# Weight sums for sixteen later Strassen squares made beside the attention and kept in DRAM

## The chip, the cores and the metric

The kernel runs on one core of a Trainium2 chip. The metric is device time of one execution in microseconds (us). The kernel before took 2009.71 us, the median of three runs (2009.61 to 2010.11). About 0.2% (4 us) is what a measurement of this kernel can tell from no change.

## The reference, cut to what matters

One transformer block over 256 tokens of width 4096, in float32:

```python
h = rmsnorm(x, norm_w)
u = h @ w_in                       # mLSTM q,k,v,o,z and attention q,k,v,gates,z
y_ml = mlstm(conv(u)) * sigmoid(ml_o) * silu(ml_z)
y_ns = sparse_attention(u) * silu(ns_z)
x = x + concat(y_ml, y_ns) @ w_out
x = x + sigmoid(x @ ple_gate) * (p @ ple_proj)
```

Nearly all of the arithmetic is in the products of 256 x 4096 activations with weight matrices of 4096 rows. The weights are read from DRAM once.

## The kernel before, in words

**Three matmuls for each product.** TensorE takes a rounded float32 type, so each operand is split into a rounded part and the rest. For a weight tile `raw`, ScalarE (ACT) writes the rounded part `whi` (line L1542) and VectorE (DVE) writes `wlo` = `raw` - `whi` (L1543). Activations lie split in SBUF as `sh` and `sl`, the stationary operands. A product is whi x sh, whi x sl and wlo x sh, all issued at L1256.

**Units.** The weights come in tiles of 128 x 2 x 512 floats (512 KB). The program is a queue of *units*, one tile each. While TensorE (PE) works on unit n, ACT and DVE split unit n + 3 (`LOOK = 3`). `whi` and `wlo` have four buffers each, `raw` has six (`RAWB = 6`). Loads of `raw` are issued on the SyncE queue (L1532) in the order of the units, each as soon as one of the six tiles is free; a tile is free when DVE has written its `wlo`.

**Groups and plans.** 1024 output columns (pairs of 512) make a group; it has 16 steps, one for each pair of 128-row blocks `kp`. Groups P1 to P5 are input projections, -6 to -1 the gates, 0 to 3 multiply by `w_out`, 4 to 7 by `ple_gate`. `PLANS[g]` writes out the order of a group's steps by hand. A step is of one of two kinds:

- `C`, plain: two units of 12 matmuls, 24 in all.
- *mixed square*: a Strassen-like 2 x 2 block product with seven block products in place of eight: four units `a1`, `a2`, `c1`, `c2` of 3, 6, 6 and 6 matmuls, 21 in all. Unit `a1` splits half a tile (L1549 on ACT, L1550 on DVE). Units `c1` and `c2` split sums of the same two raw tiles; DVE makes the sums in place with four adds of 128 x 512 (L1343, L1344, L1346, L1347), so both tiles stay held until `c1` and `c2` are split. The order is `a1 a2 C C' c1 c2`: a plain step stands between, and two of the four adds follow each of its splits. Below, "m/C" is such a mixed square with its plain step, and 3/2 is the mixed square of kp 3 with the plain step of kp 2.

A mixed square also needs *mixed* activations (sums of activation blocks), stationary tiles of their own that `t_mix` or `t_stat` makes once for each kp and each set of activations (`HOMES` says where they lie).

**The middle.** Between P4 and P5, eight single column blocks (128 units of 12 matmuls, L944 and L946) run beside the sparse attention and the mLSTM, which are written as generators that take one step for each unit; POOL's queue carries their small transfers. At the start of each group, DVE works off the result of the group before in a burst (L1161 to L1165, L1228, L1242 or L1245), between the splits.

**Names the change touches.** `RAWB`, `held_raw` (how many raw tiles are taken), `load`, `a_units`, `c_units`, `PLANS`, `HOMES`, and the condition in `t_stat` that says which chunks get mixed activations.

Of the kernel before, what the change touches and what calls it, by code (L numbers as in the profile page):

```python
# [36 lines left out]
LOOK = 3  # L37
RAWB = 6

# [32 lines left out]
}  # L72
HOMES["r"] = HOMES["y"]
PLANS[-1] = PLANS[3] = SHIFT
PLANS[0] = _plan((0, 1, 2, 3, 4, 5, 6), (9, 11, 13), (7, 8, 10), (12, 14, 15))
# [13 lines left out]
def hymba_block(ctx: ExitStack, tc: tile.TileContext, a, out: bass.AP):  # L89
# [932 lines left out]
    def cmp_unit(u):  # L1022
# [92 lines left out]
    def t_in_own(g, own):  # L1115
# [143 lines left out]
    def pair_group(g, w, stat):  # L1259
# [146 lines left out]
        def c_units(kp, last):  # L1406
            def mm1(hi, lo):
# [113 lines left out]

    raws, splits, ahead = {}, {}, {}

    def load(n):
# [7 lines left out]
        nc.sync.dma_start(raws[n], units[n]["src"])  # L1532
# [7 lines left out]
    def split_all(r, keep=False):  # L1540
        hi, lo = split_tiles()
        nc.scalar.activation(hi, r, AF.Copy)  # L1542
        nc.vector.tensor_sub(lo, r, hi)  # L1543
        held_raw[0] -= not keep
        return hi, lo
# [13 lines left out]
    def split(n):  # L1559
        if n in ahead:  # L1560
            r, hi, lo = ahead.pop(n)
            nc.vector.tensor_sub(lo, r, hi)
            held_raw[0] -= 1
            splits[n] = (hi, lo)
            return
        r = raws.pop(n, None)
        if n == 0:
# [15 lines left out]
        elif units[n]["kind"] == "narrow":  # L1583
# [138 lines left out]
```

## Time and profile before

| | us |
|---|---|
| median of three runs | 2009.71 |
| the profiled execution, its own time | 2010.0 |
| its span in the profile | 2008.1 |
| P1 to P4 | 0 to 358.9 |
| single columns beside the attention | 358.9 to 769.0 |
| P5 | 769.0 to 857.7 |
| gate groups -6, -5, -4, -3, -2, -1 begin at | 857.7, 938.1, 1016.4, 1094.8, 1173.1, 1252.1 |
| `w_out` groups 0, 1, 2, 3 begin at | 1334.0, 1419.8, 1498.1, 1576.5 |
| `ple_gate` groups 4 to 7 | 1658.5 to 2008 |

The profiled execution is 0.3 us over the median of the runs. How to read the rows: a timeline row is start, length (us), engine, line, operation, output <- input, how many in a row. A row of a windows view is the length of the stretch, then busy time (and number of instructions) of PE, PEld (weight loads), DVE, ACT and POOL, the granted clock, the share of the DMA engines and GB/s. A matmul row's mean (some 380 ns) overlaps its neighbours; the pitch of 512 columns is read from the chain.

### The profile page before, as it was taken

What the parts mean: (1) busy time and instruction counts of PE and PEld (TensorE: products, weight loads), DVE (VectorE), ACT (ScalarE), POOL (GpSimd) and SP (SyncE); (2) the same over time, 40 slices, a digit from 0 to 9 for tenths busy, and PEclk for the clock granted to TensorE, in tenths of its full rate; (3) what the DMA queues carried; (4) which work ended last, traced back from release to release, by engine and by line L of the source; (5) the groups of instructions that cost most, each with busy time, mean ns of one, the idle gap of its engine ahead of it and who ended that gap; (6) DMA issues with size and microseconds to landing.
All of it is one profiled execution on the core that took longest, in us unless ns stands there. A gap on an engine that the chain in (4) does not pass through costs nothing.

```text
span 2008.1 us, 27076 instructions
## 1 busy us (share of the span) xinstructions
PE 1997.0 (99%) x9640; PEld 1741.0 (87%) x9640; DVE 1699.6 (85%) x2166; ACT 1229.5 (61%) x1620; POOL 67.2 (3%) x133
## 2 busy tenths in 40 slices
PE   9999999999999999999999999999999999999998
PEld 7887888888888888888888888888888888888887
DVE  7987799676667758868999999989999997988998
ACT  7775566566666465666566666666555555565664
POOL 0000000011011000000000000000000000000000
PEclk9999999999999999999999999999999999999999
DMA  9867766665545665765666667666656674666664
GB/s 368 274 223 252 264 208 222 209 193 165 166 152 172 212 197 178 240 212 203 220 216 212 218 206 235 202 218 251 215 209 222 213 236 156 227 213 236 211 235 149
DMA packets 124712, 432.21 MB, mean 215 GB/s; under 512 B 15490, under 2 KB 16938, under 8 KB 124576
## 3 DMA queue, kind: packets, MB, share of 16 engines
q1 hardware_dynamic: 114336, 409.45, 60.1%
q0 software_dynamic: 10096, 21.01, 3.7%
q8 instruction: 76, 1.25, 0.3%
q14 instruction: 60, 0.49, 0.1%
q10 hardware_dynamic: 144, 0.02, 0.0%
HBM read 421.97 MB, written 7.92 MB: 214 GB/s over the span
## 4 chain that ended last, share of the span: by engine, by line
PE 95%; DVE 2%; ACT 1%; DMA 1%; issue 0%; SPq 0%; DVEq 0%; ACTq 0%
PE mm L1256 43%; PE sd L1256 29%; PE mm L944 11%; PE mm L946 5%; DVE wlo L1543 1%; PE sd L645 1%; PE sd L1035 1%; PE sd L849 1%; PE sd L285 1%; PE sd L632 0%; DMA xn<-in_x 0%; PE sd L551 0%; ACT whi L1542 0%; DMA raw<-in_w_ip 0%; PE sd L599 0%
## 5 line engine op out<-in xcount | busy, mean ns | idle before, releaser
L1542 ACT ACTIVATE whi<-raw 128x1024 fp32r<-128x1024 f32 x805 | 845.8, 1056 | 620.5 <-PE mm L1256 143.0
L1543 DVE TENSOR_TENSOR wlo<-raw,whi 128x1024 fp32r<-128x1024 f32 x805 | 977.5, 1222 | 221.6 <-ACT whi L1542 212.7
L1256 PE MATMUL mm<-whi,sh 128*128 128x512 f32 x1219 | 379.6, 382 | 0.4 <-ACT whi L1571 0.4
L1256 PE MATMUL mm<-wlo,sh 128*128 128x512 f32 x1219 | 376.6, 379 | 1.1 <-DVE wlo L1543 1.0
L1256 PE MATMUL mm<-whi,sl 128*128 128x512 f32 x1219 | 376.1, 379 | 0.0
L1256 PEld LDWEIGHTS mm<-wlo,sh 128*128 128x128 f32 x1219 | 229.8, 189 | 35.2 <-DVE wlo L1543 3.1
L1256 PEld LDWEIGHTS mm<-whi,sh 128*128 128x128 f32 x1219 | 228.3, 189 | 35.7 <-issue 2.3
L1256 PEld LDWEIGHTS mm<-whi,sl 128*128 128x128 f32 x1219 | 230.6, 189 | 32.7
L1256 PE MATMUL sd<-whi,sh 128*128 128x512 f32 x687 | 217.9, 379 | 0.0
L1256 PE MATMUL sd<-whi,sl 128*128 128x512 f32 x687 | 217.5, 378 | 0.0
L1256 PE MATMUL sd<-wlo,sh 128*128 128x512 f32 x687 | 217.5, 378 | 0.0
L944 PE MATMUL mm<-whi,sh 128*128 128x512 f32 x512 | 156.7, 388 | 0.0
L946 PE MATMUL mm<-wlo,sh 128*128 128x512 f32 x512 | 152.3, 379 | 0.0
L944 PE MATMUL mm<-whi,sl 128*128 128x512 f32 x512 | 152.3, 379 | 0.0
L1256 PEld LDWEIGHTS sd<-wlo,sh 128*128 128x128 f32 x687 | 129.9, 189 | 18.4
L1256 PEld LDWEIGHTS sd<-whi,sl 128*128 128x128 f32 x687 | 129.9, 189 | 18.4
L1256 PEld LDWEIGHTS sd<-whi,sh 128*128 128x128 f32 x687 | 129.5, 189 | 18.1
L1256 PE MATMUL sd<-whi,cb 128*128 128x512 f32 x456 | 143.0, 379 | 0.0
L1256 PE MATMUL mm<-whi,cb 128*128 128x512 f32 x392 | 126.6, 379 | 0.3 <-DVE cb L817 0.3
L946 PEld LDWEIGHTS mm<-wlo,sh 128*128 128x128 f32 x512 | 96.8, 189 | 13.7
L944 PEld LDWEIGHTS mm<-whi,sl 128*128 128x128 f32 x512 | 96.8, 189 | 13.7
L944 PEld LDWEIGHTS mm<-whi,sh 128*128 128x128 f32 x512 | 93.1, 189 | 11.6
(323 smaller groups left out, 2070.9 us busy)
## 6 DMA issues: line engine op xcount, KB each, us to landing
raw<-in_w_gate SPq DMA_DIRECT2D x192, 512.0 KB, 4.3
raw<-in_w_ip SPq DMA_DIRECT2D x160, 512.0 KB, 4.5
raw<-in_w_in SPq DMA_DIRECT2D x128, 512.0 KB, 3.5
raw<-in_w_out SPq DMA_DIRECT2D x128, 512.0 KB, 4.3
raw<-in_ple_gate SPq DMA_DIRECT2D x128, 512.0 KB, 4.2
raw<-in_w SPq DMA_DIRECT2D x16, 512.0 KB, 4.8
cb<-cb_d POOLq DMA_DIRECT2D x22, 256.0 KB, 5.2
u<-in_xt SPq DMA_DIRECT2D x8, 512.0 KB, 6.8
```

The costliest lines, as they stand in the source:

```text
L285: nc.tensor.transpose(p[:, i, :], u[:, t, i * 128:(i + 1) * 128], idn)
L645: MM(o[t][:, h, :], ptb[i][:, b, s, :], v[:, s, b, g * 128:(g + 1) * 128], start=(h == 0 and b == 0 and s == 0), stop=False)
L849: nc.tensor.transpose(pp[i // 2][:, i % 2, t * 128:(t + 1) * 128], src[:, t, k:k + 128], idn)
L944: MM(box["ps"][t], s[c][:, k, t * 128:(t + 1) * 128], paired(m[:, j]), start=st, stop=False)
L946: MM(box["ps"][t], sh[c][:, k, t * 128:(t + 1) * 128], paired(lo[:, j]), start=False, stop=last)
L1035: MM(o[64 * kv:64 * kv + 60], xq[l // 8][:, l % 8, 60 * kv:60 * kv + 60], raw[:, j, 256 * kv:256 * kv + 256], start=(l == 0), stop=(l == 31))
L1256: MM(o, s, m, start=acc.i == 0, stop=acc.i == acc.n - 1)
L1542: nc.scalar.activation(hi, r, AF.Copy)
L1543: nc.vector.tensor_sub(lo, r, hi)
```

## The change

1. **Sums ahead of time.** A generator `t_sums` runs after P4, one step for each unit beside the attention. For each of 16 later (group, kp) it loads the two weight tiles on POOL's queue, adds them on DVE (the same four adds), and stores the two sum tiles to a DRAM buffer `sum_d`, also on POOL's queue.
2. **Two of the six raw tiles are lent** to `t_sums` while it runs (tag `raws`). A list `free` says which tile came free first, and the next load takes that one; single columns take only the other four.
3. **A new step `q`**: a mixed square whose sums come from `sum_d`. Its four units are four loads (half a tile, a tile, two sum tiles), each released as soon as it is split; no plain step stands between, and DVE makes no sums for it. There are 16, two in each of groups -5, -4, -3, -2, -1, 1, 2, 3.
4. **One mixed square more** in those eight groups, kp 15 in six of them, kp 1 in -1 and 3. Kp 13 and, in the six, kp 1, 5 or 7 turn from the old kind into `q`. For it kp 15 gets mixed activations: set "x" by a `t_mix` about the end of P5, set "y" in `t_stat` at group 0.

```diff
-RAWB = 6
+RAWB, RAWS = 4, 2
+PLANS.update({g: _seq("0", "3/2", "5/4", "q13", "7/6", "9/8", "q1", "11/10", "15/12", "14") for g in (-4, -3, -2, 2)})
+PLANS[1] = _seq("0", "9/2", "11/4", "q13", "3/6", "5/8", "q7", "1/10", "15/12", "14")
+PLANS[-5] = _seq("0", "7/2", "9/4", "q13", "11/6", "3/8", "q5", "1/10", "15/12", "14")
+PLANS[-1] = PLANS[3] = _seq("0", "3/2", "5/4", "q1", "7/6", "9/8", "11/10", "q13", "12", "14", "15")
...
-                if 2 * c + half in MIXED and c >= 4:
+                if c >= 4 and (2 * c + half in MIXED or 2 * c + half == 15 and flag[0] == "y"):
...
+    def t_sums():
+        while "own-8" not in done or free.count("raws") < RAWS:
+            yield "wait"
+        for _ in range(RAWS):
+            free.remove("raws")
+        for g, kp in sum_d:
+            w = a["w_gate"][g + 6] if g < 0 else a["w_out"][g]
+            r0, r = (wk.tile([128, 2, 512], F32, tag="raws", name="raws", bufs=RAWS) for _ in range(2))
+            nc.gpsimd.dma_start(r0, w[kp, 0])
+            nc.gpsimd.dma_start(r, w[kp, 1])
+            for _ in range(4):
+                yield
+            nc.vector.tensor_add(r0[:, 1], r0[:, 1], r0[:, 0])
+            nc.vector.tensor_add(r0[:, 0], r0[:, 0], r[:, 0])
+            yield
+            nc.vector.tensor_add(r[:, 0], r[:, 0], r0[:, 1])
+            nc.vector.tensor_add(r[:, 1], r[:, 1], r[:, 0])
+            yield
+            nc.gpsimd.dma_start(sum_d[g, kp][:, 0:2], r0)
+            nc.gpsimd.dma_start(sum_d[g, kp][:, 2:4], r)
+            yield
+        free.extend(["raws"] * RAWS)
...
+            dry.extend([t_fetch((9,), "x"), t_fetch((11, 3, 5, 1), "x", "ml1"), t_mix((15,), "x", "x0m")])
...
-            unit(w[kp, 0], split1, mm1, kp, True)
+            unit(w[kp, 0][:, 1:2] if summed else w[kp, 0], split1, mm1, kp, True)
...
+            if summed:
+                for i, (mm, f) in enumerate(((mm1, None), (mm2, post))):
+                    unit(sum_d[g, kp][:, 2 * i:2 * i + 2], split_and_sum, mm, post=f)
...
+            elif kind == "q":
+                a_units(kp, True)
+                c_units(kp, i == marks, True)
...
+        tag = "raw" if units[n]["kind"] == "wide" else free[0]
+        free.remove(tag)
```

How instructions stand then, at the places that matter.

DVE in group -4, before, the mixed squares 5/4 and 7/6 (L1550 is `a1`; two of the L1543 are `a2` and `C`, one is `C'`, two are `c1` and `c2`; L1343 to L1347 are the sums):

```order
L1550 TENSOR_TENSOR wlo<-raw,whi 128x512
L1543 TENSOR_TENSOR wlo<-raw,whi 128x1024 x2
L1343 TENSOR_TENSOR raw<-raw 128x512
L1344 TENSOR_TENSOR raw<-raw 128x512
L1543 TENSOR_TENSOR wlo<-raw,whi 128x1024
L1346 TENSOR_TENSOR raw<-raw 128x512
L1347 TENSOR_TENSOR raw<-raw 128x512
L1543 TENSOR_TENSOR wlo<-raw,whi 128x1024 x2
L1550 TENSOR_TENSOR wlo<-raw,whi 128x512
L1543 TENSOR_TENSOR wlo<-raw,whi 128x1024 x2
L1343 TENSOR_TENSOR raw<-raw 128x512
```

DVE at the same place after the change (L1613 for L1550, L1605 for L1543, L1386 to L1390 for the sums), from the sums of 5/4 on:

```order
L1386 TENSOR_TENSOR raw<-raw 128x512
L1387 TENSOR_TENSOR raw<-raw 128x512
L1605 TENSOR_TENSOR wlo<-raw,whi 128x1024
L1389 TENSOR_TENSOR raw<-raw 128x512
L1390 TENSOR_TENSOR raw<-raw 128x512
L1605 TENSOR_TENSOR wlo<-raw,whi 128x1024 x2
L1613 TENSOR_TENSOR wlo<-raw,whi 128x512
L1605 TENSOR_TENSOR wlo<-raw,whi 128x1024 x3
L1613 TENSOR_TENSOR wlo<-raw,whi 128x512
L1605 TENSOR_TENSOR wlo<-raw,whi 128x1024 x2
L1386 TENSOR_TENSOR raw<-raw 128x512
```

Between 5/4 and 7/6 stands q13 now: one half split and three whole ones, and no add among them.

The loads of raw tiles on the SyncE queue; before, all 192 of the gate groups are one row:

```order
L1532 DMA raw<-in_w_ip 128x1024 x57
L1532 DMA raw<-in_w_in 128x1024 x128
L1532 DMA raw<-in_w_ip 128x1024 x32
L1532 DMA raw<-in_w_gate 128x1024 x192
L1532 DMA raw<-in_w_out 128x1024 x128
```

and after the change, through group -4:

```order
L1591 DMA raw<-in_w_gate 128x1024 x20
L1591 DMA raw<-in_w_gate 128x512
L1591 DMA raw<-in_w_gate 128x1024
L1591 DMA raw<-sum_d_13_125 128x1024 x2
L1591 DMA raw<-in_w_gate 128x1024 x8
L1591 DMA raw<-in_w_gate 128x512
L1591 DMA raw<-in_w_gate 128x1024
L1591 DMA raw<-sum_d_1_126 128x1024 x2
```

Each q takes four loads, 1.75 MB, where a mixed square of the old kind takes two of 512 KB.

POOL's queue beside the attention after the change (L1067 and L1068 load, L1077 and L1078 store; L391 is one of the attention's own transfers); before, only the attention's transfers stand there:

```order
L1067 DMA raws<-in_w_gate 128x1024
L1068 DMA raws<-in_w_gate 128x1024
L391 DMA mrow_d<-mrow 8x256
L1077 DMA sum_d_13_125<-raws 128x1024
L1078 DMA sum_d_13_125<-raws 128x1024
```

A store waits at the head of POOL's queue until DVE has made its sums, and the attention's transfers behind it wait too.

More of the change, by code (lines that the diff above doesn't have):

```diff
@@ L37 @@
 LOOK = 3
-RAWB = 6
+RAWB, RAWS = 4, 2
+BUFS = {"raw": RAWB, "raws": RAWS}
 MIXED = (3, 5, 7, 9, 11, 13)
@@ L52, in _plan, with _seq @@
     return p + [("C", k) for k in tail]
+def _seq(*items):
+    p = []
+    for x in items:
+        if x[0] == "q":
+            p.append(("q", int(x[1:])))
+        elif "/" in x:
+            m, k = x.split("/")
+            p += _plan((), (int(m),), (int(k),), ())
+        else:
+            p.append(("C", int(x)))
+    return p
 PROJ = [("p", 0), ("p", 1)]
@@ L69 @@
     "w": {9: ("nat1", 0), 11: ("nat1", 1), 3: ("b", 0), 5: ("b", 1), 13: ("a", 0), 7: ("a", 1)},
[2 rows of a table removed]
[3 rows of a table added]
 }
 HOMES["r"] = HOMES["y"]
-PLANS[-1] = PLANS[3] = SHIFT
+PLANS.update({g: _seq("0", "3/2", "5/4", "q13", "7/6", "9/8", "q1", "11/10", "15/12", "14") for g in (-4, -3, -2, 2)})
+PLANS[1] = _seq("0", "9/2", "11/4", "q13", "3/6", "5/8", "q7", "1/10", "15/12", "14")
+PLANS[-5] = _seq("0", "7/2", "9/4", "q13", "11/6", "3/8", "q5", "1/10", "15/12", "14")
+PLANS[-1] = PLANS[3] = _seq("0", "3/2", "5/4", "q1", "7/6", "9/8", "11/10", "q13", "12", "14", "15")
 PLANS[0] = _plan((0, 1, 2, 3, 4, 5, 6), (9, 11, 13), (7, 8, 10), (12, 14, 15))
@@ L178, in hymba_block @@
     cb_d = {kp: drp.tile([128, 2, 4, 128], F32R, name=f"cb_d{kp}") for kp in HOMES["u"]}
+    sum_d = {(g, kp): drp.tile([128, 4, 512], F32, name=f"sum_d{g + 6}_{kp}")
+             for g in range(-5, 4) for kind, kp in PLANS[g] if kind == "q"}
     fifo, urgent, dry, sums_of_c = deque(), deque(), [], []
-    shut = [None]
+    shut, free = [None], deque()
     behind = deque()
@@ L1151, in t_in_own @@
             add(t_mlstm(1))
-            dry.extend([t_fetch((9,), "x"), t_fetch((11, 3, 5, 1), "x", "ml1")])
+            dry.extend([t_fetch((9,), "x"), t_fetch((11, 3, 5, 1), "x", "ml1"), t_mix((15,), "x", "x0m")])
     def t_out_oth(g, oth, us):
@@ L1264, in pair_group @@
         evq.extend([f"own{g}"] * 2)
-        nC, nM = (sum(1 for kind, _ in plan if kind == x) for x in "Ca")
+        nC, nM = (sum(1 for kind, _ in plan if kind in x) for x in ("C", "aq"))
         own = [[Acc(6 * nC + (0 if (t, j) == (1, 0) else 3 * nM)) for j in range(2)] for t in range(2)]
@@ L1385, in c_unit, with a_units @@
             unit(w[kp, k], split, mm, kp, post=post)
-        def a_units(kp):
+        def a_units(kp, summed=False):
             def split1(r):
                 raw[kp] = [r]
+                if summed:
+                    release(r)
                 return split_one(r)
             def split2(r):
+                if summed:
+                    return split_all(r)
                 raw[kp].append(r)
@@ L1402, in mm2, with c_units @@
                      product(own[0][1], blocks(kp)(1, 0), hi[:, 1], lo[:, 1]))
-            unit(w[kp, 0], split1, mm1, kp, True)
+            unit(w[kp, 0][:, 1:2] if summed else w[kp, 0], split1, mm1, kp, True)
             unit(w[kp, 1], split2, mm2, kp, True)
-        def c_units(kp, last):
+        def c_units(kp, last, summed=False):
             def mm1(hi, lo):
@@ L1420, in post @@
                         new_activations(g, range(2), 0)
-            unit(None, lambda _: split_and_sum(raw[kp][0], kp), mm1)
-            unit(None, lambda _: split_and_sum(raw[kp][1], kp), mm2, post=post)
+            if summed:
+                for i, (mm, f) in enumerate(((mm1, None), (mm2, post))):
+                    unit(sum_d[g, kp][:, 2 * i:2 * i + 2], split_and_sum, mm, post=f)
+            else:
+                unit(None, lambda _: split_and_sum(raw[kp][0], kp), mm1)
+                unit(None, lambda _: split_and_sum(raw[kp][1], kp), mm2, post=post)
         def p_unit(j):
@@ L1452, in p_unit @@
                               kind="pair", split=lambda r: split_all(r)))
-        marks = max(i for i, (kind, _) in enumerate(plan) if kind == "c")
+        marks = max(i for i, (kind, _) in enumerate(plan) if kind in "cq")
         for i, (kind, kp) in enumerate(plan):
@@ L1522, in hymba_block @@
     raws, splits, ahead = {}, {}, {}
+    free.extend(["raw"] * RAWB + ["raws"] * RAWS)
     def load(n):
@@ L1530, in load, with release @@
             later.popleft()()
-        raws[n] = wk.tile([128, 8, 64] if units[n]["kind"] == "narrow" else [128, 2, 512], F32, tag="raw", name="raw", bufs=RAWB)
-        nc.sync.dma_start(raws[n], units[n]["src"])
-    held_raw, now = [0], [0]
+        tag = "raw" if units[n]["kind"] == "wide" else free[0]
+        free.remove(tag)
+        raws[n] = wk.tile([128, 8, 64] if units[n]["kind"] == "narrow" else [128, 2, 512], F32, tag=tag, name="raw", bufs=BUFS[tag])
+        place[id(raws[n])] = (tag, raws[n])
+        half = units[n]["kind"] == "pair" and units[n]["src"].shape[1] == 1
+        nc.sync.dma_start(raws[n][:, 1:2] if half else raws[n], units[n]["src"])
+    now, place = [0], {}
+    def release(r):
+        free.append(place.pop(id(r))[0])
     def split_tiles():
@@ L1543, in split_all @@
         nc.vector.tensor_sub(lo, r, hi)
-        held_raw[0] -= not keep
+        if not keep:
+            release(r)
         return hi, lo
@@ L1562, in split @@
             nc.vector.tensor_sub(lo, r, hi)
-            held_raw[0] -= 1
+            release(r)
             splits[n] = (hi, lo)
@@ L1573, in split @@
             splits[n] = (hi, lo)
-            held_raw[0] -= 1
+            release(r)
             return
@@ L1587, in split @@
             splits[n] = (hl, None)
-            held_raw[0] -= 1
+            release(r)
         elif units[n]["kind"] == "pair":
@@ L1597, in load_some @@
     def load_some():
-        while loads and held_raw[0] < RAWB:
-            held_raw[0] += 1
+        while loads and ("raw" in free if units[loads[0]]["kind"] == "wide" else free):
             load(loads.popleft())
@@ L1603, in hymba_block @@
     dry.extend([t_rms(), t_mix((9, 13), "u", "x15"), t_mix((3, 5, 7), "u", "own-11")])
-    sums_of_c.append(t_mix((11,), "u", "x15"))
+    sums_of_c.extend([t_mix((11,), "u", "x15"), t_sums()])
     for n in range(LOOK):
@@ L1617, in hymba_block @@
             un["pre"]()
-        un["mm"](*splits.pop(n))
+        hl = splits.pop(n)
+        un["mm"](*hl)
         if un["kind"] == "raw":
-            held_raw[0] -= 1
+            release(hl[0])
         if un["post"]:
```

5 rows, old and new, of the table HOMES are left out of this document.

## The prediction

> **What bounds the kernel now.** I read the page's busy times first, then the waits, then the windows by stage.
>
> ```profile
> PE 1997.0 (99%) x9640; PEld 1741.0 (87%) x9640; DVE 1699.6 (85%) x2166; ACT 1229.5 (61%) x1620; POOL 67.2 (3%) x133
> PE 95%; DVE 2%; ACT 1%; DMA 1%; issue 0%; SPq 0%; DVEq 0%; ACTq 0%
> ...
> PE mm L1256 <- DVE wlo L1543: 1.0, 2, 0.6
> PE sd L632 <- ACT s L615: 0.3, 1, 0.3
> DVE wlo L1543 <- ACT whi L1542: 212.7, 196, 5.3
> ...
> 358.90:769.00 410.10, 409.80 (x2141) 362.65 (x2140) 276.33 (x473) 249.46 (x437) 39.07 (x77) 1.00 0.56 181
> 1016.40:1094.80 78.40, 78.40 (x365) 68.66 (x364) 75.38 (x85) 48.41 (x53) 0.00 (x0) 1.00 0.64 216
> 1173.10:1252.10 79.00, 78.66 (x365) 68.57 (x364) 76.04 (x91) 48.90 (x54) 0.00 (x0) 1.00 0.65 213
> 1362.00:1368.00 6.00, 6.00 (x29) 5.25 (x29) 4.56 (x8) 4.50 (x8) 0.14 (x1) 1.00 1.02 413
> ```
>
> PE is busy 99% and carries 95% of the chain that ended last. It waited for `wlo` twice, 1.0 us in all, so a removed matmul is removed time. But DVE is nearly as full in the groups with many mixed squares: 75.38 of 78.40 us in group -4, 76.04 of 79.00 in group -2. Beside the attention it is different: 276.33 of 410.10. The DMA engines run at 0.64 in a group and moved at most 413 GB/s, at a share of 1.02, in the fullest short stretch I found.
>
> So DVE's place relative to PE is the thing to follow. I call *lead* the time from the end of a `wlo` on DVE to the first matmul that reads it. Pairs of rows, DVE and then PE, in time order: the start of group -5, one mixed square later, the usual state (group -4), the start of -2, and the start of 3.
>
> ```profile
> 950.72 1.22 DVE L1543 TENSOR_TENSOR wlo<-raw,whi 128x1024 fp32r<-128x1024 f32 x1
> 952.39 0.38 PE L1256 MATMUL mm<-wlo,cb 128*128 128x512 f32 x1
> 958.52 2.51 DVE L1543 TENSOR_TENSOR wlo<-raw,whi 128x1024 fp32r<-128x1024 f32 x2
> 962.10 0.38 PE L1256 MATMUL mm<-wlo,cb 128*128 128x512 f32 x1
> 1045.38 2.51 DVE L1543 TENSOR_TENSOR wlo<-raw,whi 128x1024 fp32r<-128x1024 f32 x2
> 1050.16 0.38 PE L1256 MATMUL sd<-wlo,cb 128*128 128x512 f32 x1
> 1186.67 1.22 DVE L1543 TENSOR_TENSOR wlo<-raw,whi 128x1024 fp32r<-128x1024 f32 x1
> 1187.94 0.48 PE L1256 MATMUL sd<-wlo,cb 128*128 128x512 f32 x1 [0.34 <-DVE wlo L1543]
> 1581.99 1.21 DVE L1543 TENSOR_TENSOR wlo<-raw,whi 128x1024 fp32r<-128x1024 f32 x1
> 1584.34 0.59 PE L1256 MATMUL sd<-wlo,sh 128*128 128x512 f32 x2
> ```
>
> The leads are 952.39 - 951.94 = 0.45, 962.10 - 961.03 = 1.07, then 2.27, 0.05 and 1.1 us. The usual lead of 2.3 is eaten by the burst at each group's start. Read the same way, the least leads behind the bursts of -5, -4, -3, -2, -1, 1, 2, 3 are 0.5, 1.2, 1.2, 0.1, 0.4, 2.0, 0.5 and 1.1. Until it is back, DVE runs without a gap: one m/C took it 961.03 - 951.94 = 9.09 us and PE 962.10 - 952.39 = 9.71, a gain of 0.6.
>
> **The change part by part.**
>
> *Matmuls.* Eight groups each turn a plain step (24 matmuls) into a mixed square (21): 24 fewer. Their price is the pitch of the chain, not the overlapped mean:
>
> ```profile
> 1016.44 5.18 PE mm L1256 x24
> ```
>
> 5.18 us go, all on the path: **-5.2**.
>
> *DVE and ACT in those groups.*
>
> ```profile
> L1542 ACT ACTIVATE whi<-raw 128x1024 fp32r<-128x1024 f32 x805 | 845.8, 1056 | 620.5 <-PE mm L1256 143.0 <-DVE raw L1344 141.2 <-PE sd L1256 107.6
> L1344 DVE TENSOR_TENSOR raw<-raw 128x512 f32<-128x512 f32 x106 | 73.3, 692 | 3.7
> L1550 DVE TENSOR_TENSOR wlo<-raw,whi 128x512 fp32r<-128x512 f32 x106 | 72.6, 685 | 4.5 <-ACT whi L1549 4.5
> L1543 DVE TENSOR_TENSOR wlo<-raw,whi 128x1024 fp32r<-128x1024 f32 x805 | 977.5, 1222 | 221.6 <-ACT whi L1542 212.7
> ```
>
> A group has one old mixed square's four adds less (4 x 0.69 = 2.75) and, for a plain step's two splits, a square's half and three whole ones (+0.685 + 1.222): -0.85 us of DVE for -0.65 of PE. By work alone nothing becomes tighter: nothing on the path.
>
> *The loads behind a q* decide. Six tiles are there. In 5/4 q13 7/6, the load of 7's `a1` goes out when 5's `c1` is split, that of 7's `a2` at 5's `c2`, the plain step's at q's `a1` and `a2`, the next at q's `c1` and `c2`. A whole split lies between, once half a one: 512 KB each 1.1 us or so, 470 GB/s, over the 413 of the window above. The nearest stretch of before is the end of group -4, where five plain splits follow one another. The rows are SyncE's issues, then the DMA view in windows that hold all five, the first, the second and the last, and last a quiet stretch of the same group (1027 to 1036):
>
> ```profile
> 1085.48 5.11 SPq L1532 DMA_DIRECT2D raw<-in_w_gate  x5
> ...
> raw<-in_w_gate SPq DMA_DIRECT2D x5, 512.0 KB, 5.1
> ...
> raw<-in_w_gate SPq DMA_DIRECT2D x1, 512.0 KB, 3.4
> ...
> raw<-in_w_gate SPq DMA_DIRECT2D x1, 512.0 KB, 4.9
> ...
> raw<-in_w_gate SPq DMA_DIRECT2D x1, 512.0 KB, 5.8
> ...
> raw<-in_w_gate SPq DMA_DIRECT2D x4, 512.0 KB, 3.5
> ```
>
> A load that comes 1.2 us behind another takes 4.9 us to land, the fifth 5.8; alone, 3.5. What is allowed? Between the end of 5's `c2` and the split of 7's `a2` DVE has q's four splits and the half split of 7's `a1`: 2 x 0.685 + 3 x 1.222 = 5.04 us by the means. An m/C is 9.55 by the means and took 9.09, so 5% comes off: 4.8. ACT needs 1.06 of it: the tile must land within 3.7 us. I take 5.0, between the second load's 4.9 and the run's median 5.1: 1.3 late. The q itself wins 0.4 back (4.14 us of DVE by the same working, 21 x 0.216 = 4.53 of PE). So each q costs D = 0.9 us of lead. The ends are 3.5 (D below zero, a cost of nothing) and 5.8, which the plain tile behind would have: 4.2 allowed, 1.6 late, D = 1.2.
>
> Lost lead is no lost time while there is some. The sum, group by group: a burst's least lead, +0.6 for an m/C (0.2 to 0.9 by group), -D for a q (under zero PE waits), +0.9 for the m/C and a half until behind the second one after a q, at most 2.3; what is missing of 2.3 at a group's end is missing in the next burst. Group -5: 0.5, 1.1, q 0.2, 1.1, q 0.2, 1.1; 1.2 are missing. Group -4: 1.2 - 1.2 = 0, 0.6, q: PE waits 0.3; 0.9, q 0, 0.9; 1.4 missing. Group -3: 0.2 + 0.3 of waiting. Group -2: 0.1 - 1.4, so 1.3, and 0.2 at the q. Group -1: 0.4 - 1.4, so 1.0, and 0.2; its three plain steps at the end give all back. Groups 1, 2 and 3 begin with 2.0, 0.4 and 0.1 and reach zero nowhere. In all 0.3 + 0.5 + 1.5 + 1.2 = **+3.5**. The same working gives 0.3 for D = 0.5 and 8.8 for D = 1.3: it is steep.
>
> The page "DMA: Bandwidth & Descriptors" of the Trainium skill, section "Anatomy of one DMA", fits a DMA as 2.0 us and bytes at 436 GB/s, an estimate of 3.2 us for 512 KB; by it D is below zero, PE waits nowhere here, and the sum ends at -4.5. The quiet row (3.5) is near that, the run of five (5.1) is not.
>
> *Kp 15's mixed activations.* Those of set "x" fall on the end of P5, whose plan closes with plain steps (2.44 us of DVE for 5.18 of PE): DVE is far ahead there, nothing. Those of set "y" come in group 0:
>
> ```profile
> 1348.53 0.87 DVE L881 SCALAR_TENSOR_TENSOR sl<-sd,hnw_c,sh 128x256 fp32r<-128x256 f32 x2
> 1349.32 0.68 DVE L875 TENSOR_TENSOR sl<-s,sh 128x512 fp32r<-128x512 f32 x1
> 1350.03 0.42 DVE L888 TENSOR_TENSOR s<-s 128x256 f32<-128x256 f32 x1
> 1350.49 0.29 DVE L889 TENSOR_TENSOR s<-s 128x128 f32<-128x128 f32 x1
> 1350.82 0.29 DVE L890 TENSOR_TENSOR s<-s 128x128 f32<-128x128 f32 x1
> 1356.02 0.68 DVE L899 TENSOR_TENSOR cb<-s,cb 128x512 fp32r<-128x512 f32 x1
> ...
> 1400.18 1.22 DVE L1543 TENSOR_TENSOR wlo<-raw,whi 128x1024 fp32r<-128x1024 f32 x1
> 1401.97 0.38 PE L1256 MATMUL sd<-wlo,cb 128*128 128x512 f32 x1
> ```
>
> 0.68 + 1.00 + 0.68 come for one 0.87 to 0.95: +1.4 us, and DVE has no gap from there to the group's last `c1`, whose lead is 1401.97 - 1401.40 = 0.57. PE then waits 0.85 there, in place of the 0.3 it waits today one unit on, since the order puts three of the other small adds behind that unit now: **+0.5** (0 to 1.4).
>
> *The sums beside the attention.* 16 x 4 x 0.69 = 44 us of adds go into 133.8 us of idle DVE. The attention's one wait of PE today is the 0.3 at L632; 32 blocks of two adds, 1.4 us each, can make a small step late here and there: **+0.2** (0 to 2). The transfers must not come late either:
>
> ```profile
> cb<-cb_d POOLq DMA_DIRECT2D x22, 256.0 KB, 5.2
> out_x<-u POOLq DMA_DIRECT2D x6, 512.0 KB, 4.3
> ```
>
> A store of 4.3 and a load of some 5 us lie between one sum's last add and the next one's first, and five units of 12 matmuls (5 x 2.59 = 13 us) are there for them; the attention's small transfers behind a waiting store are issued earlier than that. 33 MB over 350 us add 97 GB/s to 181. The lent tiles leave four to the columns, whose loads have a slow pace of one each 2.59 us.
>
> **Sum**: -5.2 + 3.5 + 0.5 + 0.2 = -1.0, against the profiled 2010.0 a time of 2009.0. That execution is 0.3 over the median, so 2008.7 as a median.
>
> **The rivals.**
>
> *All is hidden* (D at most 0.5): the second load of a run lands in 4.6 us or less, as it may, since half a tile is among q's loads. -5.2 + 0.0 to 0.3 + 0.7: 2005.3. For it speaks the quiet row's 3.5, against it the 4.9 in a run. By the Trainium skill's fit above this is the outcome too.
>
> *The loads become the bound* (other side): if tiles behind a q land as the last of the run did or a little later (5.9, D = 1.3), DVE has no lead left from -5 to 3, PE waits 8.8 us, and the time is 2009.7 - 5.2 + 8.8 + 0.7 = 2014.0. It decides from D = 1.3 on; the steady 0.64 share of the DMA engines speaks against, the 470 GB/s of demand for it.
>
> *The sums hold up DVE.* If the POOL loads take over 13 us with the store, DVE stands at an add, with the next `wlo` behind it, and PE behind that once its lead is used up. One us of waiting for each of 16 sums gives 16 - 4.5: 2021. The 4.3 and 5.2 above speak against it. The page "SBUF — State Buffer" of the Trainium skill, section "SBUF: two separate sides", says that transfers issued by GpSimd can starve while DVE holds a shared port; the rows of POOL's queue above, at a DVE two thirds busy, do not show that.
>
> **How the numbers follow.** My forecast 0.52, all hidden 0.30, loads the bound 0.13, sums 0.05. The likeliest case alone spans 2005.7 to 2012. With the others 80% lies in 2005.0 to 2012.8. What can be told from no change is 0.2%, 4 us: faster means under 2005.7, most of the second case; slower over 2013.7, most of the third and the fourth.
>
> **What would show it.** PE with 24 matmuls fewer and about 4 us more waiting for `wlo`, in groups -4 to -1; loads behind a q's `c1` at some 5 us to landing; leads of nearly 0 at the starts of -2 and -1; no new waits between 359 and 769 us. Landings of 4 us there, or leads that recover between the two q, would make the prediction wrong.

## The result, and the profile after

The changed kernel takes 2022.58 us, the median of four runs (2021.87 to 2025.10); before took 2009.76 on the same chip. The ratio is 1.0066, with a 95% interval of 1.0048 to 1.0083: slower by 13 us, where 1 us less was forecast. The profiled execution took 2022.7 us, 12.7 over the one of before.

The page's first lines and the chain:

```profile
span 2020.9 us, 27307 instructions
...
PE 1999.8 (99%) x9616; PEld 1733.3 (86%) x9616; DVE 1729.8 (86%) x2222; ACT 1232.9 (61%) x1639; POOL 101.3 (5%) x197
...
PE 80%; DVE 10%; DMA 5%; ACT 3%; issue 2%; POOL 0%; ACTq 0%; DVEq 0%; POOLq 0%
```

PE has its 24 matmuls fewer, as forecast. But of the chain that ended last it carries 80% now and not 95%: DVE, the loads and ACT have 18%. The waits view says where (engine and line, what it waited for: us in total, times, longest):

```profile
ACT whi L1604 <- DMA raw<-in_w_gate: 25.1, 26, 3.4
...
ACT whi L1604 <- DMA raw<-in_w_out: 9.8, 15, 2.4
...
PE sd L1299 <- ACT whi L1604: 2.9, 5, 1.0
...
PE sd L652 <- ACT s L635: 1.9, 4, 0.8
PE sd L745 <- ACT mqk L723: 1.0, 1, 1.0
```

ACT now waits 35 us for the loads of `w_gate` and `w_out` to land; before, the waits view has no row for these loads. L652 and L745 belong to the attention and the mLSTM.

To place the loss I counted matmuls to the first one of each stage and took its start in both traces. The difference of each stage's length to before, in us; "eight groups" is -5 to -1 and 1 to 3, and a saving without new waits would be -5.2 there. P5, -6 and 4 to 7 are within 0.02 throughout (but for -0.4 in group 4 of `replan`, and +0.4 behind the last matmul of `late_q_no15`).

| kernel (below) | median us | ratio, 95% | P1 to P4 | attention | eight groups | group 0 |
|---|---|---|---|---|---|---|
| changed kernel | 2022.58 | 1.0066, 1.0048 to 1.0083 | -1.3 | +4.9 | +7.7 | +1.4 |
| `sums_only` | 2015.00 | 1.0025, 1.0015 to 1.0034 | +1.1 | +4.1 | 0.0 | 0.0 |
| `no_adds` | 2018.04 | 1.0038, 1.0023 to 1.0053 | +0.4 | 0.0 | +6.1 | +1.4 |
| `single_adds` | 2019.00 | 1.0041, 1.0026 to 1.0056 | -0.2 | +1.2 | +6.8 | +1.4 |
| `pool_adds` | 2031.01 | 1.0107, 1.0092 to 1.0122 | +0.7 | +16.8 | +7.6 | +1.4 |
| `half_loads` | 2011.64 | 1.0007, 0.9997 to 1.0017 | -0.9 | +4.1 | -5.2 | +1.4 |
| `thin_last_four` | 2014.18 | 1.0024, 1.0015 to 1.0033 | +0.4 | +3.9 | -1.7 | +1.4 |
| `thin_first_two` | 2011.60 | 1.0010, 1.0000 to 1.0019 | +0.5 | +4.9 | -4.7 | +1.4 |
| `paired_q` | 2015.54 | 1.0030, 1.0020 to 1.0040 | -0.7 | +5.1 | 0.0 | +1.4 |
| `replan` | 2050.39 | 1.0205, 1.0190 to 1.0220 | -0.1 | +1.2 | +37.0 | +2.4 |
| `late_q` | 2014.92 | 1.0027, 1.0016 to 1.0038 | +0.7 | +1.2 | +2.8 | +1.4 |
| `late_q_no15` | 2011.55 | 1.0008, 0.9999 to 1.0017 | -1.2 | +1.2 | +1.0 | 0.0 |
| `alternate_q` | 2010.03 | 1.0003, 0.9994 to 1.0012 | +0.2 | +1.2 | -2.2 | 0.0 |

The columns come from one profiled execution of each kernel, which need not be its median: that of `half_loads` was 2.3 us under it, that of `pool_adds` 5.3 us over it. In P1 to P4 no kernel changes an instruction, and one execution still differs from another by up to 1.3 us either way: that is scatter. Where PE waits, the other columns can scatter as much: the attention has the same instructions in six of these kernels (pieces of two adds) and costs 3.9 to 5.1 there, and the same plans of the eight groups give 6.1 to 7.7 in four. Where PE does not wait they are steady to 0.01 (0.0 in `sums_only` and `paired_q`).

So of the changed kernel's 12.7 us, -5.2 are the matmuls, +12.9 new waits in the eight groups (7.7 + 5.2), +4.9 the attention, +1.4 group 0, and -1.3 scatter. Windows of the changed kernel, over the attention, groups -4 and -3, and group 0 (length, then busy PE, PEld, DVE, ACT, POOL, clock, DMA share, GB/s):

```profile
357.70:772.70 415.00, 411.43 (x2140) 362.32 (x2139) 315.17 (x537) 248.85 (x437) 71.97 (x139) 1.00 0.76 260
1020.80:1100.00 79.20, 78.77 (x361) 67.64 (x361) 73.75 (x83) 48.40 (x55) 0.00 (x0) 1.00 0.66 231
1100.00:1180.40 80.40, 78.79 (x361) 67.55 (x361) 73.79 (x83) 48.46 (x55) 0.00 (x0) 1.00 0.66 231
1342.10:1429.20 87.10, 86.13 (x416) 74.66 (x415) 78.77 (x115) 53.72 (x75) 3.38 (x5) 1.00 0.66 230
```

DVE's work in group -4 fell from 75.38 to 73.75 us, and the DMA share rose only from 0.64 to 0.66: neither average shows the loss. One q does. The timelines of group -4 from 5/4's `c2` to 7/6's plain step, DVE, then ACT, then PE:

```profile
1042.47 1.22 DVE L1605 TENSOR_TENSOR wlo<-raw,whi 128x1024 fp32r<-128x1024 f32 x1
1043.61 0.68 DVE L1613 TENSOR_TENSOR wlo<-raw,whi 128x512 fp32r<-128x512 f32 x1
1044.21 3.49 DVE L1605 TENSOR_TENSOR wlo<-raw,whi 128x1024 fp32r<-128x1024 f32 x3
1047.62 0.68 DVE L1613 TENSOR_TENSOR wlo<-raw,whi 128x512 fp32r<-128x512 f32 x1
1050.72 2.52 DVE L1605 TENSOR_TENSOR wlo<-raw,whi 128x1024 fp32r<-128x1024 f32 x2 [2.42 <-ACT whi L1604]
...
1045.98 0.63 ACT L1612 ACTIVATE whi<-raw 128x512 fp32r<-128x512 f32 x1
1049.63 1.06 ACT L1604 ACTIVATE whi<-raw 128x1024 fp32r<-128x1024 f32 x1 [3.02 <-DMA raw<-in_w_gate]
...
1050.19 0.38 PE L1299 MATMUL sd<-wlo,sh 128*128 128x512 f32 x1
1050.74 0.48 PE L1299 MATMUL mm<-whi,cb 128*128 128x512 f32 x1 [0.17 <-ACT whi L1604]
1051.06 0.38 PE L1299 MATMUL mm<-whi,sh 128*128 128x512 f32 x1
...
1052.00 0.48 PE L1299 MATMUL mm<-wlo,cb 128*128 128x512 f32 x1
1052.32 0.38 PE L1299 MATMUL mm<-wlo,sh 128*128 128x512 f32 x1
```

q13 itself is split from 1043.61 to 1047.70 without a gap, and 7's `a1` follows at 1047.62 with a lead of 1050.19 - 1048.30 = 1.89 us. Then ACT stands 3.02 us for the load of 7's `a2`, DVE 2.42 behind it, and the next lead is 1052.00 - 1051.94 = 0.06, with PE waiting for `whi` and for `wlo` in turn. The matmul at 1052.32 is the sixth after the one at 1050.19: 2.13 us, where six times the pitch of 0.216 is 1.30. One q took the whole lead of 1.9, and 0.8 us of PE's time beside it. This is the step that the prediction named, at twice its price or more.

### The profile page after: what moved, and what is told of

The parts are those of the page before. It is cut to its first block, busy times and chain, and to the rows that moved or that the text cites. A ratio compares the mean times of both kernels' runs of the same rounds, so it can differ in the third digit from the quotient of the medians.

```text
span 2020.9 us, 27307 instructions
## 1 busy us (share of the span) xinstructions
PE 1999.8 (99%) x9616; PEld 1733.3 (86%) x9616; DVE 1729.8 (86%) x2222; ACT 1232.9 (61%) x1639; POOL 101.3 (5%) x197
## 4 chain that ended last, share of the span: by engine, by line
PE 80%; DVE 10%; DMA 5%; ACT 3%; issue 2%; POOL 0%; ACTq 0%; DVEq 0%; POOLq 0%
PE mm L1299 39%; PE sd L1299 22%; PE mm L964 8%; DVE wlo L1605 5%; PE mm L966 4%; DMA raw<-in_w_gate 2%; ACT whi L1604 2%; DMA raw<-in_w_out 1%; PE sd L665 1%; PE sd L1055 1%; PE sd L869 1%; DVE wlo L1625 1%; DVE raw L1386 0%; DVE sq L719 0%; PE sd L305 0%
## 5 line engine op out<-in xcount | busy, mean ns | idle before, releaser
L1605 DVE TENSOR_TENSOR wlo<-raw,whi 128x1024 fp32r<-128x1024 f32 x813 | 982.3, 1221 | 218.8 <-ACT whi L1604 210.5
L1299 PEld LDWEIGHTS mm<-whi,sh 128*128 128x128 f32 x1206 | 225.8, 189 | 35.0 <-issue 2.6
L1299 PE MATMUL sd<-wlo,sh 128*128 128x512 f32 x660 | 210.9, 379 | 0.5 <-DVE wlo L1613 0.3
L1299 PE MATMUL sd<-whi,sh 128*128 128x512 f32 x660 | 211.0, 379 | 0.0
L1299 PE MATMUL sd<-whi,sl 128*128 128x512 f32 x660 | 210.6, 378 | 0.0
L1299 PE MATMUL sd<-whi,cb 128*128 128x512 f32 x484 | 152.7, 380 | 2.9 <-ACT whi L1604 2.9
L1299 PEld LDWEIGHTS sd<-wlo,sh 128*128 128x128 f32 x660 | 124.3, 189 | 19.2 <-DVE wlo L1605 0.9
L1299 PEld LDWEIGHTS sd<-whi,sl 128*128 128x128 f32 x660 | 124.7, 189 | 17.6
L1299 PEld LDWEIGHTS sd<-whi,sh 128*128 128x128 f32 x660 | 124.4, 189 | 17.6 <-issue 0.2
L1299 PE MATMUL mm<-whi,cb 128*128 128x512 f32 x428 | 138.3, 380 | 1.1 <-ACT whi L1604 0.8
L1299 PEld LDWEIGHTS sd<-whi,cb 128*128 128x128 f32 x484 | 91.5, 189 | 17.9 <-ACT whi L1604 5.1
```

The lines of the kernel that those rows point to most:

```text
L1299: MM(o, s, m, start=acc.i == 0, stop=acc.i == acc.n - 1)
```

## Experiments

### The attention: is it the adds or the transfers?

`sums_only` has the plans of before and makes the sums for nobody:

```diff
-PLANS.update({g: _seq("0", "3/2", "5/4", "q13", ...) ...})
+PLANS[-1] = PLANS[3] = SHIFT
...
+    sum_d = {(g, kp): ... for the same 16 pairs}
...
```

> The plans of before (no step q, no extra mixed square, no mixed activations of kp 15), but the sums are still made and stored beside the attention, with four raw tiles left to the columns there. In the changed kernel the stretch up to the end of the attention takes 3.6 us more than before, group 0 1.4 more, the eight groups 7.7 more. Theory (adds on DVE in the attention's way): the 3.6 stay and nothing else, about 2013.4. Rival (the sums are free, all of the loss is behind the q): about 2009.8.

It measured 2015.00: +4.1 in the attention, 0.0 in the eight groups, 0.0 in group 0. The loss beside the attention stands alone, and needs no q. (The first of the two expected sums leaned on the changed kernel's P1 to P4, which was 1.3 quick.)

`no_adds` leaves the adds out of the changed kernel, and keeps its transfers and the four raw tiles of the columns:

```diff
-            nc.vector.tensor_add(r0[:, 1], r0[:, 1], r0[:, 0])
-            nc.vector.tensor_add(r0[:, 0], r0[:, 0], r[:, 0])
             yield
-            nc.vector.tensor_add(r[:, 0], r[:, 0], r0[:, 1])
-            nc.vector.tensor_add(r[:, 1], r[:, 1], r[:, 0])
             yield
```

> The changed kernel without the four adds of each sum: the tiles are loaded and stored unsummed, so the transfers and the four raw tiles stay and the values are other ones. Theory (DVE's adds delay the attention's small steps): the 3.6 us go, about 2019. Rival (the transfers on POOL's queue, or the four tiles, delay it): stays at about 2022.6.

`single_adds` makes one add for each unit in place of two:

```diff
-            for _ in range(4):
+            for _ in range(3):
                 yield
             nc.vector.tensor_add(r0[:, 1], r0[:, 1], r0[:, 0])
+            yield
             nc.vector.tensor_add(r0[:, 0], r0[:, 0], r[:, 0])
             yield
             nc.vector.tensor_add(r[:, 0], r[:, 0], r0[:, 1])
+            yield
             nc.vector.tensor_add(r[:, 1], r[:, 1], r[:, 0])
```

> The changed kernel with the four adds of a sum in four steps of one add each, in place of two of two (and a wait of three units in place of four before them). Theory (a small step of the attention waits for the whole block of two adds, 1.38 us): each wait of PE there shrinks by up to 0.69 us, the attention's +4.9 to about +1.5: 2019. Rival (it is DVE's total that counts): stays near 2022.6.

Both came as the theory had it, at 2018.04 and 2019.00. The windows over the attention of `no_adds` and of `single_adds`, each with its row for the wait at L652:

```profile
359.40:769.50 410.10, 409.81 (x2141) 362.64 (x2140) 276.39 (x473) 249.20 (x437) 71.41 (x138) 1.00 0.79 263
...
PE sd L652 <- ACT s L635: 0.3, 1, 0.3
```

```profile
358.80:770.10 411.30, 410.20 (x2141) 362.73 (x2140) 310.38 (x533) 248.81 (x437) 71.91 (x139) 1.00 0.76 258
...
PE sd L652 <- ACT s L635: 1.1, 2, 0.7
```

Without the adds the stretch is 410.10 us long, to the hundredth that of before, at 263 GB/s in place of 181 and with 32 stores on POOL's queue: transfers and tiles cost nothing. With nearly the same DVE work in pieces of 0.69 us the loss is 1.2, not 4.9. So it is the length of the piece in DVE's row that counts, and not DVE's total.

One more rival is that the attention's transfers come late behind stores that wait for the sums. But POOL's queue waits longer for the adds in `single_adds` (145.6 and 85.7 us at the two stores) than in the changed kernel (136.9 and 44.6), and the loss is smaller. That rules it out as the main cause.

How a piece makes PE wait can be read where a copy of the softmax (L637 before, L657 after) is followed by a split of DVE. The rows are DVE before; DVE, ACT and PE in the changed kernel; DVE in `single_adds`:

```profile
629.68 1.23 DVE L1562 TENSOR_TENSOR wlo<-raw,whi 128x1024 fp32r<-128x1024 f32 x1 [0.97 <-ACT whi L1557]
```

```profile
630.74 0.68 DVE L1074 TENSOR_TENSOR raws<-raws 128x512 f32<-128x512 f32 x1
631.45 0.69 DVE L1075 TENSOR_TENSOR raws<-raws 128x512 f32<-128x512 f32 x1
632.06 1.22 DVE L1625 TENSOR_TENSOR wlo<-raw,whi 128x1024 fp32r<-128x1024 f32 x1
...
634.82 0.69 DVE L630 TENSOR_REDUCE mx<-s 128x2 f32<-128x512 f32 x1
...
635.54 0.51 ACT L635 ACTIVATE s<-s,mx 128x256 f32<-128x256 f32 x1 [0.25 <-DVE mx L630]
...
636.25 0.41 PE L652 MATMUL sd<-idn,s 128*128 128x128 f32 x2 [0.55 <-ACT s L635]
```

```profile
504.00 0.68 DVE L1077 TENSOR_TENSOR raws<-raws 128x512 f32<-128x512 f32 x1
505.13 1.22 DVE L1627 TENSOR_TENSOR wlo<-raw,whi 128x1024 fp32r<-128x1024 f32 x1 [0.45 <-ACT whi L1622]
```

Before, DVE stands idle for 0.97 us at such a place. One add of 0.69 fits into that, and 0.45 us of waiting are still there in `single_adds`; two adds do not fit. In the changed kernel the split follows them at once, every step behind it is late, the maximum of the softmax (L630) among them, and 3 us later ACT and then PE stand waiting for it. The other waits of PE were not all followed back in this way.

`pool_adds` gives the adds to POOL:

```diff
-            nc.vector.tensor_add(r0[:, 1], r0[:, 1], r0[:, 0])
+            nc.gpsimd.tensor_add(r0[:, 1], r0[:, 1], r0[:, 0])
...
```

> The changed kernel with the adds of the sums on POOL in place of DVE. Theory (the adds are in the way because DVE works in order): the 3.6 us before the end of the attention go, about 2019. Rival (POOL's adds slow DVE's or hold up POOL's transfers for the attention): 2022 or more.

This became slower, 2031.01, as the rival had it. The first fence is an add on DVE in the changed kernel; the second is a split on DVE in `no_adds`, over the attention. The third is of `pool_adds`: the add on POOL, the same split over the attention, the window over the attention, and a wait of PE (the rows of groups give us in total and mean ns):

```profile
L1071 DVE TENSOR_TENSOR raws<-raws 128x512 f32<-128x512 f32 x16 | 10.9, 683 | 0.0
```

```profile
L1601 DVE TENSOR_TENSOR wlo<-raw,whi 128x1024 fp32r<-128x1024 f32 x85 | 103.7, 1223 | 83.2 <-ACT whi L1600 83.1
```

```profile
L1071 POOL TENSOR_TENSOR raws<-raws 128x512 f32<-128x512 f32 x16 | 21.3, 1334 | 30.5 <-DMA raws<-in_w_gate 18.6 <-DMA raws<-in_w_out 11.9
...
L1605 DVE TENSOR_TENSOR wlo<-raw,whi 128x1024 fp32r<-128x1024 f32 x85 | 111.9, 1324 | 69.8 <-ACT whi L1604 69.8
...
359.60:786.50 426.90, 416.17 (x2140) 364.80 (x2140) 310.83 (x473) 248.97 (x437) 171.11 (x203) 0.99 0.74 253
...
PE sd L617 <- DVE s L628: 4.9, 5, 2.3
```

An add takes POOL 1334 ns where DVE needs 683, and over the stretch in which POOL adds, DVE's own split goes from 1223 to 1324 ns on average. DVE's 473 instructions take 310.83 us in place of the 276.39 of `no_adds`, and PE waits up to 2.3 us for a small step. The run does not tell how much of the +16.8 is due to the slower DVE alone. The page "SBUF — State Buffer" of the Trainium skill, section "Who interferes with whom", says that a DVE instruction with two SBUF inputs contends with a GpSimd instruction that reads SBUF; these rows agree.

### The eight groups: is it the loads behind a q?

`half_loads` marks the six loads behind each q:

```diff
+        if n in thin:
+            nc.gpsimd.memset(raws[n][:, 0:1], 0.0)
+            nc.sync.dma_start(raws[n][:, 1:2], units[n]["src"][:, 1:2])
+            return
```

> The changed kernel, but the six loads behind each q bring half a tile (256 KB); the other half is set to zero by POOL, so a part of the weights is left out. Theory (the bytes of loads in flight together make the second one land 6 us after its issue where 3.7 are allowed): landings of 4 us or less behind a q, PE's waits in the eight groups fall from 12.9 us to 2 or less, about 2012. Rival (the four splits in a row on ACT and DVE, or a fixed latency, and not the bytes): the waits stay, 2020 or more.

It measured 2011.64. The window over group -4 and the wait row that had 25.1 us:

```profile
1019.00:1096.70 77.70, 77.70 (x361) 68.04 (x361) 74.59 (x84) 49.92 (x55) 6.29 (x12) 1.00 0.61 197
...
ACT whi L1613 <- DMA raw<-in_w_gate: 0.4, 1, 0.4
```

PE is busy in 77.70 of 77.70 us. Every one of the eight groups is 0.65 us shorter than before, the three matmuls, and the 12.9 us of waits are gone with the bytes, though DVE and ACT split the same q in the same order. That rules out the rival, the four splits in a row or a fixed latency.

`thin_last_four` and `thin_first_two` halve only some of the six:

```diff
-            thin.update([...][:6])
+            thin.update([...][2:6])     # thin_last_four; [:2] in thin_first_two
```

> As half_loads, but of the six loads behind each q only the last four bring half a tile (the other half zero, a part of the weights is left out); the first two are whole. Theory (loads in flight share the DMA engines, so that the later ones slow the second): the second lands in some 4 us, most of the 12.9 us of waits goes, 2013 to 2015. Rival (each queue of loads is served in order, the second is late because of the first and of what is ahead): it still lands at 5.5 to 6 us, and the waits stay, 2019 or more.

> The complement of thin_last_four: of the six loads behind each q only the first two bring half a tile (the other half zero, a part of the weights is left out), the last four are whole. Theory (loads in flight share the DMA engines): the four whole ones still slow the second and are late themselves: the second lands at 4 to 5 us, the third at 5 or more, and 3 to 8 us of the 12.9 us of waits stay, 2014 to 2019. Rival (the second is late because of its own bytes and the first's): the waits go as in half_loads, about 2011.6.

The DMA views of the windows around the issue of 7's `a2` in group -4, the second load: changed kernel, `thin_last_four`, `thin_first_two`:

```profile
raw<-in_w_gate SPq DMA_DIRECT2D x1, 512.0 KB, 5.8
```

```profile
raw<-in_w_gate SPq DMA_DIRECT2D x1, 512.0 KB, 5.0
```

```profile
raw<-in_w_gate SPq DMA_DIRECT2D x1, 256.0 KB, 3.0
```

For all 16 q I took each load's issue and landing from the trace; medians in us, in order of issue (they go out 0, 1.3, 1.9, 3.0, 4.2 and 5.3 us after the first in the changed kernel):

| | 1st | 2nd | 3rd | 4th | 5th | 6th |
|---|---|---|---|---|---|---|
| changed kernel | 4.2 | 5.9 | 6.6 | 6.8 | 6.8 | 6.9 |
| `thin_last_four` | 3.6 | 5.2 | 5.3 | 4.7 | 4.3 | 3.8 |
| `thin_first_two` | 2.9 | 2.9 | 4.0 | 4.9 | 5.4 | 5.4 |
| `half_loads` | 2.9 | 2.9 | 3.1 | 2.9 | 3.0 | 3.0 |

The first came out as expected in time (2014.18; 9.5 of the 12.9 us gone): halving loads that are issued *behind* the second makes it land 0.6 us earlier, though at 5.2 and not in some 4 us. In the second the rival came out (2011.60): I had expected 3 to 8 us of waits to stay, and 0.4 stayed. So both count, but not equally. Most of the second load's time is its own bytes and those of the first (5.9 to 2.9 us); the four whole loads behind land as late as 5.4 us, and PE hardly waits for them.

`paired_q` keeps the bytes and changes the pace. A plain step goes between each q's second and third unit:

```diff
-PLANS.update({g: _seq("0", "3/2", "5/4", "q13", "7/6", "9/8", "q1", "11/10", "15/12", "14") ...})
+PLANS.update({g: _seq("0", "3/2", "5/4", "q13/6", "7/8", "9/10", "q1/12", "11/14", "15") ...})
```

> The changed kernel with a plain step between each q's second and third unit (q13/6, then 7/8 and so on), so that the loads behind a q go out at the pace of TensorE; there is then no plain step left for kp 15, which stays plain in six groups, and the eight groups have the matmuls of before. DVE has 5.5 us less to do in each than before. Theory (only the run of loads at DVE's pace behind a bare q is late): no wait of PE in the eight groups, their sum like before (+0.0); the attention's +4.9 (here with the first stage some +3.6) and group 0's +1.4 stay: about 2015.5. Rival (reading sums from DRAM costs at any place, since it is 43% more loads): waits stay, 2019 or more.

2015.54, and the eight groups are at 0.00 each. The rows are its loads of `w_gate` between 942 and 1338 us, ACT's waits for them and for the sums, and the window over group -4:

```profile
raw<-in_w_gate SPq DMA_DIRECT2D x142, 512.0 KB, 5.1
...
ACT whi L1606 <- DMA raw<-in_w_gate: 0.7, 2, 0.5
ACT whi L1606 <- DMA raw<-sum_d: 18.1, 15, 2.4
...
1020.95:1099.30 78.35, 78.35 (x365) 68.61 (x364) 70.39 (x78) 48.34 (x53) 0.00 (x0) 1.00 0.68 237
```

The sum came out, but not for the reason given. The loads stay late: the six behind a paired q land after 5.5 to 6.4 us in the median, and ACT now waits 18.1 us for the sums. PE does not wait all the same; DVE has only 70.39 us of work in 78.35 here, where it had 73.75 in the changed kernel, and so more slack to make a delay good. So the 32 reloads of sums cost no time in a plan with that much slack on DVE, and the rival is out. Whether it is the slack or the slower pace behind a q that saves it, this run cannot tell, since the pairing changes both. And because the pairing uses up a plain step, kp 15's matmuls are not saved.

### Can the plan be mended?

`replan` pairs one q and puts the bare one right behind it, with single adds:

```diff
+PLANS.update({g: _seq("0", "3/2", "q13/4", "q1", "5/6", "7/8", "9/10", "11/12", "15/14") for g in (-4, -3, -2, 2)})
...
+PLANS[-1] = PLANS[3] = _seq("0", "3/2", "q1/4", "5/6", "7/8", "9/10", "q13/12", "11/14", "15")
...
```

> Single adds, and plans with one q paired with a plain step and the bare q right behind it, where DVE has gained 2.75 us of lead (0 3/2 q13/4 q1 5/6 7/8 9/10 11/12 15/14); groups -1 and 3 have no bare q at all. PE has the same 24 matmuls fewer than before. Theory (a bare q costs some 1.9 us of lead, and only where the lead is under that PE waits): at the bare q the lead is 2.3, four mixed squares with plain steps bring it back before the next burst: waits in the eight groups 2 us or less, sum of the groups -3 to -5; with group 0's +1.4 and the attention's +1.5 about 2010. Rival (the loads stay late whatever the lead): groups +5 or more, about 2018.

A clear miss, 2050.39, for a reason that neither theory had:

```profile
PE mm L1302 <- DVE sl L905: 11.2, 2, 6.2
PE sd L1302 <- DVE u L1207: 3.4, 2, 1.7
```

Now a mixed square is the last step of six groups, and in -1 and 3 one plain step stands behind the last one, where three stood. Those plain steps had hidden DVE's work on the mixed results, and PE waits for that work (L1207, and L905 behind -1 and 3) at the next group's start. The run says nothing on the lead.

`late_q` leaves head and tail as they were, and moves both q back; `late_q_no15` gives up kp 15 in set "y" and the changed plans of groups 1 and 2:

```diff
+PLANS.update({g: _seq("0", "3/2", "5/4", "7/6", "q13", "9/8", "11/10", "15/12", "q1", "14") for g in (-4, -3, -2, 2)})
...
```

> Single adds, and the two bare q moved later in the group, one behind four mixed squares (lead back at 2.3 in most groups), one ahead of the last plain step (0 3/2 5/4 7/6 q13 9/8 11/10 15/12 q1 14). Theory (a bare q costs 1.9 us of lead and no time where the lead is there; a plain step behind gives 1.4 per unit back): waits of the eight groups fall from 12 us to 2 or 4, their sum to -1 to -3; with the attention's 1.2 and group 0's 1.4 about 2010. Rival (where the q stands does not matter): the groups stay at +7, 2019.

> As late_q, but kp 15 gets no mixed activations in group 0, and groups 1 and 2 have the plans of before (12 sums, 18 matmuls fewer). Theory (group 0's 1.4 are the extra mixing on DVE alone): group 0 is back at +0.0, groups 1 and 2 too, the attention below 1.2: about 2008 to 2009. Rival (group 0's loss comes from what group -1 leaves behind): group 0 stays at +1.4.

`late_q`: waits in the eight groups fall from 12.0 (`single_adds`) to 8.0, not to 2 to 4, and the time is 2014.92 and not 2010: half a miss. `late_q_no15` is clear on its own question: group 0 is back at 0.0, so its 1.4 us are the extra mixing of kp 15. Its time, 2011.55, misses the 2008 to 2009, since the five changed groups from -5 to -1 still wait much as in `late_q`, 4.9 us in all. `alternate_q` changes only every other group:

```diff
+PLANS[-5] = _seq("0", "7/2", "9/4", "11/6", "q13", "3/8", "5/10", "15/12", "q1", "14")
+PLANS[-3] = _seq("0", "3/2", "5/4", "7/6", "q13", "9/8", "11/10", "15/12", "q1", "14")
+PLANS[-1] = PLANS[3] = _seq("0", "3/2", "5/4", "7/6", "q1", "9/8", "11/10", "q13", "12", "14", "15")
...
```

> The plans of late_q in groups -5, -3, -1 and 3 alone (eight sums in single adds, 12 matmuls fewer, no kp 15 in group 0); groups -4, -2, 1 and 2 have the plans of before. Theory (a group's missing lead is paid in the next group's burst, and a group of the old kind gives the lead back): waits in each changed group at most 0.3 us and its sum -0.4 to -0.65, the untouched groups 0 to +1.3 where a low burst (-2) follows; attention +0.6; in all -1 to +0.5, 2009 to 2010. Rival (each q costs time where it stands): the changed groups at +0.5 or more each, 2012.

```profile
1095.90:1173.60 77.70, 77.70 (x362) 68.04 (x361) 73.64 (x82) 49.48 (x55) 0.00 (x0) 1.00 0.70 233
```

That is group -3, with both q bare and PE never waiting. The four changed groups are at -0.30, -0.65, -0.65 and -0.65, the others at 0.0. The same plan in the same group waits 0.8 us in `late_q`, where group -4 is changed too. So a bare q in this place was free in three of four groups that follow one of the old kind, and cost 0.35 us in the fourth, -5, right behind its first q. That fits the theory that `late_q` pays for lead which changed groups fail to hand on; where exactly each lost it I did not follow. In the profiled execution 2.6 us of matmuls are saved, less 0.35 of waits and the attention's 1.2, which eight sums cost as well as sixteen (0.6 was expected): 1.1 us. The medians do not show that: the whole kernel is at 2010.03 us, 1.0003 (0.9994 to 1.0012). No version beats before by what can be told.

## Why the prediction was wrong

- **Matmuls, -5.2**: right, to the hundredth (`half_loads`: eight times -0.65).
- **The loads behind a q, +3.5**: the mechanism was right (the second load of a run, more bytes asked for at once, lead lost, PE waiting once it is gone), and the step that failed is the landing time. "I take 5.0" was read off one run of five loads at a spacing of 1.2 us; it was 5.9. Behind a q the third load goes out 0.6 us after the second, and six follow instead of five; with the four behind the second halved it was 5.2. By the prediction's own working D is then 5.9 - 3.7 - 0.4 = 1.8 in place of 0.9. The prediction called the sum steep and had 8.8 us for D = 1.3; the same working with 1.8 gives some 17 (an estimate), and 12.9 were measured. Why it is less than 17 stays open. The upper end of the range, D = 1.2, gave the row's slowest load, 5.8, to the plain tile behind only and not to the tile that is tight.
- **The sums, +0.2 (0 to 2)**: wrong by its step "44 us of adds go into 133.8 us of idle DVE". Idle time was the wrong measure; the length of one piece in DVE's row was the right one. Measured: 3.9 to 5.1 for pieces of two adds, 1.2 for single adds, 0.0 for none. The transfers' part, at nothing, was right, though the loads on POOL's queue took 6.3 to 6.7 us in the median and not some 5.
- **Kp 15 in group 0, +0.5 (0 to 1.4)**: its upper end. The whole 1.4 us arrive as waits, not 0.85 less the old 0.3:

```profile
1403.22 0.48 PE L1299 MATMUL sd<-wlo,sh 128*128 128x512 f32 x1 [0.33 <-DVE wlo L1613]
...
1411.62 0.70 PE L1299 MATMUL sd<-wlo,cb 128*128 128x512 f32 x2 [0.52 <-DVE wlo L1605]
```

  The reading looked at the last `c1` alone; PE waits at a half split (L1613), 8 us earlier, as well.
- **Set "x", the DVE balance of a group**: right. P5 is at 0.00, and with the loads thinned PE waits no longer in any of the eight groups than before.
- **The rivals**: "the loads become the bound" is what came, with the attention's adds on top. "The sums hold up DVE" had the wrong mechanism (late transfers): DVE stood at an add once, for 1.3 us. "All is hidden" drew on the quiet row's 3.5 us, and a load behind a q does not come quietly. The estimate of 3.2 us for 512 KB by the page "DMA: Bandwidth & Descriptors" of the Trainium skill, section "Anatomy of one DMA", rests on a fit for transfers issued from GpSimd, and the loads here are issued by SyncE; the quiet row is near it, the medians from the second load behind a q on (5.9 to 6.9 us) are not.

## What to carry to other kernels

Ask of each load when its buffer comes free, when its data is needed, and how many loads are in flight in between: a change that frees several buffers in quick succession makes a burst of loads, and the average DMA share (0.64 before, 0.66 after) says nothing of it. On an engine whose instructions run one behind the other, as DVE's do in these rows, place extra work by the length of one piece against the slack of what stands right behind it, not by idle time in total. And where a lead is lost, look for the place that gives it back before the next one needs it: the plans of -5, -3, -1 and 3 cost 0.35 us of waiting together with only these groups changed, and 3.4 us in `late_q`, with all eight changed.

## What the runs showed of the hardware

- Six loads of 512 KB at a spacing of 0.6 to 1.3 us land 4.2 to 6.9 us after issue, 256 KB each in 2.9 to 3.1. A load is slowed by loads issued behind it (5.9 against 5.2 us).
- An add of 128 x 512 takes POOL 1.33 us or more against DVE's 0.68, and over the stretch with POOL's adds DVE's two-input subtractions (L1605) are 8% longer on average.
- A wait of PE costs more than itself: the matmul at 1050.74 was followed only at 1051.06, after 0.32 us, where the pitch is 0.216, and the one at 1052.00 after 0.32 us again.
